# The experts' x in rows of their own, their slots one group ahead, and whole matrices as items

## The chip, the cores and the metric

The kernel runs on one core of a Trainium2 chip; the other seven have nothing to do. The metric is the device time of one launch in microseconds, as the median of several runs. The profile is of one execution. In what follows PE is the matrix engine (TensorE), DVE VectorE, ACT ScalarE, POOL GpSimd and SP the queue that issues most transfers.

## What is computed

256 tokens of 1024 features pass through two blocks of two layers each, all in float32. The first block holds recurrent, attention and MLP layers; it is not touched here. In the second block each of the two layers is a mixer (latent attention in layer 0, pooled means in layer 1), a layer norm, a sum over experts and a layer norm. There are 64 experts, and a token goes to two of them:

```
f = mla_mixer(...) if i == 0 else pool_mixer(...)
x = layer_norm(DEEPNORM_ALPHA * x + f, ln_g[i, 0], ln_b[i, 0])
f = hier_moe(x, ...)                 # gate * (silu(x @ w1[e]) * (x @ w3[e])) @ w2[e], over 2 experts e of 64
x = layer_norm(DEEPNORM_ALPHA * x + f, ln_g[i, 1], ln_b[i, 1])
```

An expert's w1 and w3 are 1024 x 256 and its w2 is 256 x 1024, a mebibyte each. All 64 experts of both layers are computed, so 384 such matrices, 403 MB, come from memory once.

## The kernel before

Each engine's instructions run in the order in which the program writes them. For the experts (function moe) they are done in 16 groups of four, `for g in range(16)`, in each of two layers. An expert has 32 slots for rows, so a group has 128. The steps of a group on PE, with the lines of their products:

- gather (L1406): the rows of the group's tokens are picked and turned in one, by a product of x, which is the stationary operand, with a one-hot matrix G of tokens by slots. DVE makes G of the slots' numbers (L1397). A product takes 128 features of x by 128 slots; there are 8 chunks of features and 2 blocks of tokens, and the trace has two records for each product in float32, so 32. The chunks are those features whose number is the same modulo 8 (`xk = x.rearrange("p b (q k) -> p b k q", k=8)`), because the weights' rows are laid over the partitions as "(p k)". So a chunk of x is read in steps of eight elements.
- up (L1444): products of w1 and w3 with the gathered rows, then tanh and two products on ACT and DVE (L1448 to L1451) that give h.
- back (L1429): G times the gates is Gg (DVE, L1425); two transposes of it make GT, the weighted way back.
- down: two transposes of h (L1459), a copy to hT (ACT, L1461), the products with w2 (L1470) to Y, and the products of GT with Y (L1479) that add into the accumulators of both token blocks.

The order around a group's end is: up of group g, then on DVE G of group g + 1, gather of g + 1, Gg of g + 1, back, and then down of group g. In group GAIN (6) the norm's gain and shift are put on x (affine), and alpha * x is added to the sum (L1586). After the products of group OVER (8) stands the code for experts with more than 32 rows, behind a branch on a number that the router finds; in the profiled execution none of its instructions run.

The weights come as items of 1 MB in the order of use, a list that stream_items writes. For w1 and w3 an item is half of the rows of two experts: `w[l, e:e + 2].rearrange("e (p k) f -> p e (k f)", k=8)[:, :, h * 1024:(h + 1) * 1024]`, in two pieces of 4096 bytes a partition. A w2 item is one expert's matrix, 8192 bytes in a piece. The last four items, w2 of the last group, are quarters of the columns over four experts, in pieces of 1024 bytes. There are 21 slots for items, ten in the pool that the earlier layers used and eleven that come free with the experts' phase. raw_w(key) hands out item i and has item i + 20 issued, so the transfer of an item waits until the item 21 before it has been used. On SP a transfer also waits for one of eight completion counters (DMAHW0 to 7), which are taken in turn. Between the two layers two more items bring the pooling mixer's weights.

Of the kernel before, what the change touches and what calls it, by code (L numbers as in the profile page):

```python
# [9 lines left out]
F32 = mybir.dt.float32  # L10
# [60 lines left out]
def _layout(inputs):  # L71
    """The arrays of the launch: the inputs, the small vectors also laid end to end, constants of the shapes."""
    a = {n: np.ascontiguousarray(inputs[n]) for n in _INS}
    a["rows"] = np.concatenate([a[n].reshape(-1, 128) for n in _ROWS])
    a["brows"] = np.concatenate([a[n].reshape(-1, 128) for n in _BROWS])
    a["wr"] = np.concatenate([a["moe_w_grp_2"], a["moe_w_exp_2"]], -1)
    a["br"] = np.concatenate([a["moe_b_grp_2"], a["moe_b_exp_2"]], -1)
    a["cst"], a["poolm"] = _constants()
    return a


class Kern:
# [6 lines left out]
    # ---------------------------------------------------------------- weights  # L89
    def stream_items(self):  # L90
# [59 lines left out]
        for l in range(2):  # L150
            for g in range(16):
                for h in range(2):
                    for n, w in ((1, A["moe_w1_2"]), (3, A["moe_w3_2"])):
                        for q in range(2):
                            e = 4 * g + 2 * q
                            it.append(((n, l, g, h, q), w[l, e:e + 2].rearrange("e (p k) f -> p e (k f)", k=8)
                                       [:, :, h * 1024:(h + 1) * 1024], (2, 1024)))
# [39 lines left out]
    def tick(self, ahead=1):  # L197
        """half of the next split but one: first hi, then lo."""
# [72 lines left out]
    def g_tok(self, xT, key, outs, n, splitn=1, mid=None):  # L271
        """outs[blk][j]: [128, n]: token rows, from both halves of K."""
# [18 lines left out]
    def g_feat(self, xT, key, mid=None, bank=None, end=None):  # L291
        """[128 features, 2, 256 tokens] twice, for 512 features."""
# [73 lines left out]
    def rsqrt(self, r, n):  # L366
        """r <- r ** -0.5 for r [128, n], n <= 4: a seed from the exponent, then Newton steps."""
# [57 lines left out]
    # ---------------------------------------------------------------- attention over pairs of 64-wide heads  # L425
    def attend(self, ap, pairs, scores, V, mask, outp, yts, sink=None, pre=None):
        """Softmax attention, two heads at a time, three pairs in flight. Gives the prologue and the rest."""
# [69 lines left out]
        def main(pend=None, nxt=None, ahead=1):  # L497
            """The pairs in turn; then the products out of the last are still owed. nxt() makes an attention to go on with."""
# [29 lines left out]
    # ---------------------------------------------------------------- mixer 0  # L528
    def mixer0(self):
        nc, A = self.nc, self.A  # L530
        with ExitStack() as st:
# [30 lines left out]
            def lru():  # L562
                col = self.col
                # halves of the biases, 2 * softplus(-lambda)
# [5 lines left out]
                for hf in range(2):  # L570
# [26 lines left out]
                    # tanh(z/2) = w, z = -log a: a = 2/(1+w) - 1, sqrt(1-a^2) = 2 sqrt(w)/(1+w)  # L597
# [34 lines left out]
            def forget():  # L632
                # log sigmoid, running sums, biases
# [72 lines left out]
    def pair_scores(self, qT, kT):  # L706
        """Heads 2p and 2p+1 in the two halves of the partitions of chunk p."""
# [145 lines left out]
    # ---------------------------------------------------------------- squared relu mlp  # L853
# [35 lines left out]
    # ---------------------------------------------------------------- mixer 1  # L889
    def mixer1(self, xT):  # L890
        nc, A = self.nc, self.A
        x = self.x
        with ExitStack() as st:
# [4 lines left out]
            tab = ap.tile([128, 2, 2, 2, 32], F32, name="tab")     # q or k, block, cos or sin  # L898
# [11 lines left out]
            def rope(dst, src, nh, qk, b):  # L910
                """dst, src [128, nh, 64]."""
# [11 lines left out]
            def feat(dst, tk, nch):  # L923
                """tokens x features (two blocks) to features x tokens."""
# [92 lines left out]
    def stats(self, y):  # L1017
        """mean and 1 / sqrt(var + eps) of a block of rows in parts, in steps: a seed from the exponent, Newton steps."""
# [23 lines left out]
    def both(self, gens):  # L1042
        """the generators' steps in turn; what they return."""
# [11 lines left out]
    def normed(self, y, dst):  # L1055
        """dst <- (y - mean) / sqrt(var + eps); y[block][half]."""
# [5 lines left out]
    def affine(self, g, bb):  # L1062
        """x <- x * g + b."""
        for o, v in ((ALU.mult, g), (ALU.add, bb)):
            for h in range(2):
                for b in range(2):
                    t = self.x[:, b, h * 512:(h + 1) * 512]
                    self.nc.vector.tensor_tensor(t, t, v[h], op=o)

    def router(self, rp):  # L1070
        """the router's weights times the gain of the norm before, less the mean over the rows; its bias plus that of
        the norm's shift. In steps."""
# [22 lines left out]
    def rotary(self):  # L1095
        """tables from the positions: cos, sin [128, block, 16], in steps."""
# [71 lines left out]
            # what dies first comes first: the experts' weights follow into it  # L1168
# [97 lines left out]
            # the residual's own norm  # L1266
# [16 lines left out]
    def warm(self, n):  # L1283
        """products that nothing reads, against the drop of TensorE's clock in a wait."""
# [4 lines left out]
    # ---------------------------------------------------------------- experts  # L1289
    def moe(self, l, wp, bank, y, before_last):  # L1290
        """x becomes the norm's output before gain and shift, of y[block][half]; bank: banks that are free at the start.
        The sum is returned. The router's weights are free of their columns' means, so that it can take y as it is."""
# [8 lines left out]
        # logits, token rows; feature chunk k is k, k + 8, ...  # L1301
        xk = x.rearrange("p b (q k) -> p b k q", k=8)
# [25 lines left out]
        def one_hots(v, n, k):  # L1328
            """the first k of v [128, 2, 8] from the largest on, the first of equals first: one-hot, and values."""
# [32 lines left out]
        def gates():  # L1362
            nonlocal gt, ci
            # gates
# [18 lines left out]
            # further rounds of 32 rows an expert  # L1383
# [10 lines left out]
        def gather(g, s, first=False):  # L1394
            """rows of group g: [128 features, 8, 128 slots], in halves of the features, and the one-hot slots."""
            G = wp.tile([128, 2, 4, 32], F32, name="G", bufs=1)
            tt(G, s[:, :, 4 * g:4 * g + 4, None].to_broadcast([128, 2, 4, 32]),  # L1397
               iota[:, None, None, :].to_broadcast([128, 2, 4, 32]), op=ALU.is_equal)
            Gf = G.rearrange("p b e s -> p b (e s)")
# [20 lines left out]
            return xg, G, half  # L1420

        def back(g, G):
# [386 lines left out]
```

## Time and profile before

| | us |
|---|---|
| runs: median (lowest to highest) | 1929.14 (1928.67 to 1932.13) |
| profiled execution: span from the first to the last instruction | 1926.0 |
| PE busy | 1748.4 (91%) |
| DVE busy | 749.8 (39%) |
| ACT busy | 578.8 (30%) |

The time of the profiled execution as the runs are timed isn't shown; its span lies 3.1 us below their median. The first gather of the experts starts at 920.4 us, so their phase, with the pooling mixer within it, is the last 1005 us. Of the page's groups, the costliest of this phase are the gather (252.5 us on PE, 1024 records), the products with w1 and w3 (235.6 us, 4096), those with w2 (160.6 us, 992) and the way back (118.2 us, 248). Busy time is no measure of what could be saved: an engine that waits is idle in it, and one that is slow is busy. Transfers moved 550.11 MB, 286 GB/s over the span.

### The profile page before, as it was taken

The numbers are of one execution on the slowest core, as the hardware profiler recorded it, in microseconds if no ns is written. First come the engines' busy times: TensorE is split into PE (matmuls) and PEld (weight loads), VectorE is DVE, ScalarE is ACT, GpSimd is POOL, SyncE is SP. The second block draws the span as 40 slices with busy tenths as digits, with TensorE's granted clock in tenths as the row PEclk, the third lists the DMA queues.
The fourth block names the chain that finished last, engine by engine and source line by source line (L and its number), as shares of the span: only waits on it lengthen the run. The fifth ranks groups of instructions, "written<-read, shape, count | busy, mean of one in ns | idle before, by whom it ended". The sixth has DMA issues, their size and how long they took to land. (4 is left out here: it accounts for less than half of the span.)

```text
span 1926.0 us, 29923 instructions
## 1 busy us (share of the span) xinstructions
PE 1748.4 (91%) x12712; PEld 1316.9 (68%) x12712; DVE 749.8 (39%) x1599; ACT 578.8 (30%) x1047; POOL 11.3 (1%) x22
## 2 busy tenths in 40 slices
PE   7999999999999999999888897888998878878886
PEld 7998899989878899877554554555475455545554
DVE  6886576556675655585210111101151111110112
ACT  5644445444564544466111100000021110000001
POOL 0000000000000000000000000000000000000000
PEclk9999999999999999999888889888998879898898
DMA  8544355554524455556899999999989999999993
GB/s 278 179 152 150 117 170 197 187 184 155 196 66 153 147 195 184 177 213 256 341 356 411 415 384 403 409 419 422 418 360 359 378 415 412 386 406 413 422 421 115
DMA packets 160611, 550.11 MB, mean 286 GB/s; under 512 B 9660, under 2 KB 33551, under 8 KB 144463
## 3 DMA queue, kind: packets, MB, share of 16 engines
q1 hardware_dynamic: 158175, 539.18, 73.2%
q0 software_dynamic: 2144, 8.66, 1.2%
q8 instruction: 104, 1.70, 0.3%
q14 instruction: 44, 0.36, 0.0%
q10 hardware_dynamic: 144, 0.21, 0.0%
HBM read 546.97 MB, written 1.05 MB: 285 GB/s over the span
## 5 line engine op out<-in xcount | busy, mean ns | idle before, releaser
L237 DVE TENSOR_TENSOR wl<-wr,wh 128x1024 fp32r<-128x1024 f32 (+4 forms) x268 | 309.5, 1197 | 119.7 <-ACT wh L234 76.1
L1406 PE MATMUL b<-G,x 128*128 128x128 f32 x1024 | 252.5, 418 | 64.6 <-DVE G L1397 64.5
L1406 PEld LDWEIGHTS b<-G,x 128*128 128x128 f32 x1024 | 247.0, 335 | 78.7 <-issue 78.0
L234 ACT ACTIVATE wh<-wr 128x1024 fp32r<-128x1024 f32 (+4 forms) x268 | 265.1, 1037 | 103.9 <-DVE wl L237 72.3
L1444 PE MATMUL b<-wr,xg 128*32 128x256 f32 x4096 | 235.6, 388 | 2.3 <-ACT xg L1414 2.3
L1444 PEld LDWEIGHTS b<-wr,xg 128*32 128x32 f32 x4096 | 129.6, 112 | 113.1 <-issue 28.0
L1470 PE MATMUL b<-wr,hT 128*32 128x512 f32 x992 | 160.6, 806 | 18.0 <-ACT hT L1461 18.0
L320 PE MATMUL a<-wh,yh 128*128 128x512 f32 x416 | 168.0, 404 | 2.7 <-ACT yh L334 2.7
L320 PE MATMUL a<-wh,yl 128*128 128x512 f32 x416 | 165.1, 397 | 0.6 <-DVE yl L335 0.6
L320 PE MATMUL a<-wl,yh 128*128 128x512 f32 x416 | 164.1, 394 | 0.0
L1449 DVE SCALAR_TENSOR_TENSOR th<-th,b 128x256 f32<-128x256 f32 x32 | 13.5, 421 | 326.4 <-ACT th L1448 326.4
L304 PE MATMUL b<-xh,wl 128*128 128x256 f32 x448 | 121.9, 282 | 0.0
L304 PE MATMUL b<-xh,wh 128*128 128x256 f32 x448 | 121.7, 281 | 0.0
L1470 PEld LDWEIGHTS b<-wr,hT 128*32 128x32 f32 x992 | 36.3, 143 | 124.8 <-issue 96.2
L1479 PE MATMUL a<-Y,GT 128*128 128x512 f32 x248 | 118.2, 618 | 0.0
L1448 ACT ACTIVATE th<-b 128x256 f32<-128x256 f32 x32 | 12.3, 384 | 326.9 <-PE b L1444 326.9
L304 PE MATMUL b<-xl,wh 128*128 128x256 f32 x448 | 110.3, 282 | 0.0
L1475 DVE COPY Y<-b 128x512 f32<-128x512 f32 x31 | 21.4, 692 | 206.9 <-PE b L1470 206.9
L320 PEld LDWEIGHTS a<-wh,yh 128*128 128x128 f32 x416 | 78.1, 188 | 23.3 <-ACT yh L334 4.5
L1479 PEld LDWEIGHTS a<-Y,GT 128*128 128x128 f32 x248 | 42.0, 189 | 75.7 <-issue 30.5
L320 PEld LDWEIGHTS a<-wh,yl 128*128 128x128 f32 x416 | 78.1, 188 | 22.5 <-DVE yl L335 3.9
L304 PE MATMUL a<-xh,wh 128*128 128x256 f32 x320 | 90.0, 290 | 1.5 <-ACT xh L348 1.1
(460 smaller groups left out, 2533.2 us busy)
## 6 DMA issues: line engine op xcount, KB each, us to landing
wr<-in_moe_w SPq DMA_DIRECT2D x372, 1024.0 KB, 15.4
wr<-in_mlp_w_up SPq DMA_DIRECT2D x32, 1024.0 KB, 5.3
wr<-in_mlp_w_down SPq DMA_DIRECT2D x32, 1024.0 KB, 4.9
wr<-in_xa_w_kv SPq DMA_DIRECT2D x16, 1024.0 KB, 5.3
wr<-in_xa_w_q SPq DMA_DIRECT2D x8, 1024.0 KB, 4.9
wr<-in_xa_w_o SPq DMA_DIRECT2D x8, 1024.0 KB, 5.0
wr<-in_cd_w_in SPq DMA_DIRECT2D x8, 1024.0 KB, 4.9
wr<-in_moe_w POOLq DMA_DIRECT2D x8, 1024.0 KB, 7.2
```

Source lines behind the costliest of these rows:

```text
L234: nc.scalar.activation(hi[:, s], r[:, s], AF.Copy)
L237: nc.vector.tensor_tensor(lo[:, s], r[:, s], hi[:, s].bitcast(F32), op=ALU.subtract)
L304: nc.tensor.matmul(o[f // 2][:, f % 2, :], wt[c][:, kk, f * 128:(f + 1) * 128], xT(a, h * 4 + kk), start=(h == 0 and kk == 0 and a == 0 an ...
L320: nc.tensor.matmul(acc[b][hf], yT[a][:, chunk, b * 128:(b + 1) * 128], wt[c][:, j, hf * 512:(hf + 1) * 512], start=(first and a == 0 and c ...
L1406: nc.tensor.matmul(ps[:, k], xk[:, b, 4 * i + k], Gf[:, b], start=(b == 0), stop=(b == 1))
L1444: nc.tensor.matmul(ps[32 * e:32 * e + 32, which], xg[:, k, 32 * e:32 * e + 32], w(e, k), start=(which == 0 and k == 0), stop=(k == 7), ski ...
L1448: nc.scalar.activation(th, ps[:, 0], AF.Tanh, scale=0.5)
L1449: stt(th, th, 1.0, ps[:, 0], op0=ALU.add, op1=ALU.mult)
L1470: nc.tensor.matmul(y[hf][32 * e:32 * e + 32], hT[:, c, 32 * e:32 * e + 32], w(c)[:, hf * 512:(hf + 1) * 512], start=(c == 0), stop=(c == 1 ...
L1475: nc.vector.tensor_copy(Y[:, 512:], y[1])
L1479: nc.tensor.matmul(acc[b][hf], GT[:, b * 128:(b + 1) * 128], Y[:, hf * 512:(hf + 1) * 512], start=first, stop=end, skip_group_check=True)
```

## The change

There are four parts. Comments and doc strings are dropped as well, which moves the lines' numbers.

1. x is kept in another order of columns in the experts' phase: chunk k of the features lies in 128 columns of its own. So the gather and the router's transposes read x in a row, and the steps that write x or take it by halves (the copy ahead of the router, affine, the product with alpha) go over it in steps of 128 elements.
2. G and Gg of group g + 2 are made on DVE at the end of group g's down, one group earlier. For this G and Gg are functions of their own (slots, weighted).
3. The transposes of h (turned, out of down) stand between gather and back.
4. An item of w1 or w3 is a whole matrix of one expert, 8192 bytes a partition. The order of products in up is now w1, first half of the rows, w1, second half, w3, w3, where it was w1, w3, w1, w3; and four items are taken at once.

```diff
@@ stream_items
-                for h in range(2):
-                    for n, w in ((1, A["moe_w1_2"]), (3, A["moe_w3_2"])):
-                        for q in range(2):
-                            e = 4 * g + 2 * q
-                            it.append(((n, l, g, h, q), w[l, e:e + 2].rearrange("e (p k) f -> p e (k f)", k=8)
-                                       [:, :, h * 1024:(h + 1) * 1024], (2, 1024)))
+                for n, w in ((1, A["moe_w1_2"]), (3, A["moe_w3_2"])):
+                    for e in range(4):
+                        it.append(((n, l, g, e), w[l, 4 * g + e].rearrange("(p k) f -> p k f", k=8), (8, 256)))
@@ affine
-    def affine(self, g, bb):
+    def affine(self, g, bb, half=None, as_=lambda t: t):
+        half = half or (lambda b, h: self.x[:, b, h * 512:(h + 1) * 512])
...
-                    t = self.x[:, b, h * 512:(h + 1) * 512]
-                    self.nc.vector.tensor_tensor(t, t, v[h], op=o)
+                    t = half(b, h)
+                    self.nc.vector.tensor_tensor(t, t, as_(v[h]), op=o)
@@ moe
-        xk = x.rearrange("p b (q k) -> p b k q", k=8)
+        xk = x.rearrange("p b (k q) -> p b k q", k=8)
+        xn = x.rearrange("p b (k q) -> p b q k", k=8)
+        half_x = lambda b, h: xn[:, b, 64 * h:64 * h + 64]
+        by8 = lambda t: t.rearrange("p (q k) -> p q k", k=8)
...
-                nc.scalar.activation(x[:, b, h * 512:(h + 1) * 512], y[b][h], AF.Copy)
+                nc.scalar.activation(half_x(b, h), by8(y[b][h]), AF.Copy)
@@ moe, parts
-            def get(n, h):
+            def get(n):
+                w = []
+
                 def f():
-                    w = [self.raw_w(n, l, g, h, q) for q in range(2)]
-                    return lambda e, k: w[e // 2][:, e % 2, (k % 4) * 256:(k % 4 + 1) * 256]
+                    if not w:
+                        w.extend(self.raw_w(n, l, g, e) for e in range(4))
+                    return lambda e, k: w[e][:, k]
                 return f
-            return [(n // 2, range(4 * h, 4 * h + 4), get(n, h)) for h in range(2) for n in (1, 3)]
+            return [(n // 2, range(4 * h, 4 * h + 4), f) for n, f in ((1, get(1)), (3, get(3))) for h in range(2)]
@@ moe, the loop over groups
             if g < 15:
-                xg, G, half = gather(g + 1, s1, g < GAIN)
+                xg, half = gather(G, g < GAIN)
                 if g:
                     half(1)
-                    GT = back(g + 1, G)
+            if g != OVER:
+                hT = turned(h)
+            if 0 < g < 15:
+                GTn = back(Gg)
...
+            if g < 14 and g != OVER - 1:
+                G = slots(g + 2, s1)
+                Gg = weighted(g + 2, G)
             if g < 15:
+                GT = GTn
                 h = up(g + 1, xg, parts(g + 1), fill=fill)
```

Three places show what stands where. The first is DVE around the end of up of group 2 in layer 0, where h is the group's activation, xg the gathered rows and Y the products with w2. Before:

```order
L1449 SCALAR_TENSOR_TENSOR th<-th,b 128x256 [waits Activation_49]
L1451 SCALAR_TENSOR_TENSOR h<-th,b 128x128x2 [waits DVE_49]
L1397 TENSOR_TENSOR G<-r_s_8831,keep 128x256
L1412 TENSOR_SCALAR xg<-b,pcol 128x128 [waits Activation_49] x4
L1425 TENSOR_TENSOR Gg<-G,r_gt 128x256 [waits DVE_49]
L1475 COPY Y<-b 128x512 [waits PE_49]
L1449 SCALAR_TENSOR_TENSOR th<-th,b 128x256 [waits Activation_49]
```

With the change:

```order
L1486 COPY Y<-b 128x512 [waits PE_49]
L1398 TENSOR_TENSOR G<-r_s_8831,keep 128x256
L1404 TENSOR_TENSOR Gg<-G,r_gt 128x256 [waits DVE_49]
L1457 SCALAR_TENSOR_TENSOR th<-th,b 128x256 [waits Activation_49]
L1459 SCALAR_TENSOR_TENSOR h<-th,b 128x128x2 [waits DVE_49]
L1422 TENSOR_SCALAR xg<-b,pcol 128x128 [waits Activation_49] x4
L1486 COPY Y<-b 128x512 [waits PE_49]
```

G stood behind h and Gg behind the copies of xg, each just ahead of the products on PE that read it. Both now stand behind the copy of Y, ahead of the activations th and h of a group that comes before their use.

The second place is PE at the end of up of group 1 in layer 0: gather of group 2 (G, x), transposes of Gg and of h, and the first products with w2 (wr holds an item). Before:

```order
L1406 MATMUL b<-G,x 128x128 x16
L1429 MATMUL b<-keep,Gg 128x128 x2
L1459 MATMUL b<-keep,h 128x128 x2
L1470 MATMUL b<-wr_8692,hT 32x512
L1470 MATMUL b<-wr,hT 32x512 x3
L1470 MATMUL b<-wr_8692,hT 32x512
```

With the change:

```order
L1416 MATMUL b<-G,x 128x128 x16
L1466 MATMUL b<-keep,h 128x128 x2
L1437 MATMUL b<-keep,Gg 128x128 x2
L1481 MATMUL b<-wr_8692,hT 32x512
L1481 MATMUL b<-wr,hT 32x512 x3
L1481 MATMUL b<-wr_8692,hT 32x512
```

The transposes of h are now ahead of those of Gg. The number of products is the same.

The third place is PE in group 0 of layer 0, with the product of ones in which the router counts rows (r_M). Before:

```order
L1406 MATMUL b<-G,x 128x128 x8
L1444 MATMUL b<-wr,xg 32x256 x32
L1385 MATMUL b<-r_M,ones 128x64 x2
L1406 MATMUL b<-G,x 128x128 x8
L1444 MATMUL b<-wr,xg 32x256 x32
```

With the change:

```order
L1416 MATMUL b<-G,x 128x128 x8
L1452 MATMUL b<-wr,xg 32x256 x16
L1386 MATMUL b<-r_M,ones 128x64 x2
L1416 MATMUL b<-G,x 128x128 x8
L1452 MATMUL b<-wr,xg 32x256 x48
```

The first half of w3 stood ahead of the second half of the gather; now only the first half of w1 does, and no item has been used up at that point, since an item of w1 serves both halves.

## Rows read from the trace of the kernel before

**Rows 1.** The page: span of the profiled execution.
```profile
span 1926.0 us, 29923 instructions
```

**Rows 2.** Stretches: us, busy of each engine (instructions), PE's clock, DMA share, GB/s.
```profile
932.00:1400.00 468.00, 397.63 (x3228) 236.56 (x3228) 62.22 (x132) 44.62 (x99) 0.00 (x0) 0.87 0.99 401
1510.00:1880.00 370.00, 314.01 (x2528) 190.36 (x2521) 45.98 (x96) 33.76 (x74) 0.00 (x0) 0.88 1.01 411
```

**Rows 3.** PE's waits in 1510 to 1880: for whom, us in total, times, longest.
```profile
PE b L1406 <- DVE G L1397: 28.8, 13, 4.3
PE b L1429 <- DVE Gg L1425: 19.1, 12, 2.4
```

**Rows 4.** Waits of SP's queue in 850 to 1926, the same columns.
```profile
SPq L180 <- PE b L1470: 285.8, 30, 17.5
SPq L180 <- DMA wr<-in_moe_w: 105.9, 76, 3.3
```

**Rows 5.** One group on PE: start, us, engine, line, operation, idle before it.
```profile
1760.64 7.86 PE L1406 MATMUL b<-G,x 128*128 128x128 f32 x32 [1.96 <-DVE G L1397]
1769.70 0.41 PE L1429 MATMUL b<-keep,Gg 128*128 128x128 f32 x2 [1.21 <-DVE Gg L1425]
1770.86 5.24 PE L1470 MATMUL b<-wr,hT 128*32 128x512 f32 x32 [0.53 <-ACT hT L1461]
1776.04 3.81 PE L1479 MATMUL a<-Y,GT 128*128 128x512 f32 x8
1779.78 7.11 PE L1444 MATMUL b<-wr,xg 128*32 128x256 f32 x128
```

**Rows 6.** Loads of x on PE (ns min/median/max), and eight products of the mixer.
```profile
L1406 PEld LDWEIGHTS b<-G,x x1024: 312/336/341, 920.3 to 1881.6; 128*128 128x128 f32 x171
...
L1618 PEld LDWEIGHTS a<-wr,x x16: 190/192/192, 1407.8 to 1411.3; 128*128 128x128 f32 x16
...
L1311 PEld LDWEIGHTS a<-keep,x x16: 187/193/207, 1421.4 to 1423.5; 128*128 128x128 f32 x16
...
1408.01 1.05 PE L1618 MATMUL a<-wr,x 128*128 128x128 f32 x8
```

**Rows 7.** Short stretches by kind of item: w2, w1/w3, between layers, the last four.
```profile
1820.00:1827.50 7.50, 5.76 (x25) 5.20 (x23) 1.02 (x2) 1.37 (x3) 0.00 (x0) 0.73 1.01 425
1800.00:1817.50 17.50, 15.54 (x171) 7.01 (x164) 1.97 (x4) 0.98 (x2) 0.00 (x0) 0.96 1.03 420
1400.00:1432.50 32.50, 31.43 (x205) 27.43 (x203) 19.98 (x83) 10.35 (x16) 0.00 (x0) 1.00 1.02 423
1880.00:1887.50 7.50, 5.76 (x30) 3.34 (x33) 1.02 (x2) 0.77 (x2) 0.00 (x0) 0.77 1.07 365
1887.50:1895.00 7.50, 7.50 (x101) 4.15 (x93) 0.69 (x1) 1.79 (x3) 0.00 (x0) 1.00 0.35 121
```

**Rows 8.** Starts: layer 0's first group, between the layers, after the branch, the end.
```profile
920.37 4.08 PE L1406 MATMUL b<-G,x 128*128 128x128 f32 x16 [0.94 <-DVE G L1397]
925.06 3.75 PE L1444 MATMUL b<-wr,xg 128*32 128x256 f32 x64 [0.61 <-ACT xg L1414]
...
1393.79 3.64 PE L1470 MATMUL b<-wr,hT 128*32 128x512 f32 x32 [0.53 <-ACT hT L1461]
...
1432.73 1.66 PE L1406 MATMUL b<-G,x 128*128 128x128 f32 x6 [0.94 <-DVE G L1397]
...
1711.96 0.42 DVE L1397 TENSOR_TENSOR G<-r_s,keep 128x256 f32<-128x256 f32 x1 [6.46 <-PEq L1525]
...
1911.17 1.07 PE L1500 MATMUL b<-wr,hT 128*32 128x256 f32 x16
```

**Rows 9.** Stretches with the transfers in part idle: layer 0's start, layer 1's start.
```profile
925.00:927.50 2.50, 2.44 (x44) 1.15 (x48) 1.61 (x9) 0.78 (x4) 0.00 (x0) 1.00 0.18 75
927.50:930.00 2.50, 2.50 (x34) 1.78 (x24) 1.48 (x10) 0.00 (x0) 0.00 (x0) 1.00 0.78 233
1432.50:1442.50 10.00, 9.16 (x88) 6.99 (x89) 3.33 (x20) 1.23 (x4) 0.00 (x0) 1.00 0.37 139
```

More of the change, by code (lines that the diff above doesn't have):

```diff
@@ L1392, in gates, with slots @@
             nc.vector.tensor_copy(ci, cm)
-        def gather(g, s, first=False):
+        def slots(g, s):
             G = wp.tile([128, 2, 4, 32], F32, name="G", bufs=1)
@@ L1398, in gather, with weighted @@
                iota[:, None, None, :].to_broadcast([128, 2, 4, 32]), op=ALU.is_equal)
+            return G
+        def weighted(g, G):
+            Gg = wp.tile([128, 2, 4, 32], F32, name="Gg", bufs=1)
+            tt(Gg, G, gt[:, :, 4 * g:4 * g + 4, None].to_broadcast([128, 2, 4, 32]), op=ALU.mult)
+            return Gg
+        def gather(G, first=False):
             Gf = G.rearrange("p b e s -> p b (e s)")
@@ L1419, in gather, with back @@
             half(0)
-            return xg, G, half
-        def back(g, G):
-            Gg = wp.tile([128, 2, 4, 32], F32, name="Gg", bufs=1)
-            tt(Gg, G, gt[:, :, 4 * g:4 * g + 4, None].to_broadcast([128, 2, 4, 32]), op=ALU.mult)
+            return xg, half
+        def back(Gg):
             Gg = Gg.rearrange("p b e s -> p b (e s)")
@@ L1453, in up, with turned @@
             return h
-        def down(g, h, GT, acc, getw2, first, end, fill=()):
+        def turned(h):
             ps = self.pb([128, 2, 128])
@@ L1461, in down @@
             nc.scalar.activation(hT, ps, AF.Copy)
+            return hT
+        def down(g, hT, GT, acc, getw2, first, end, fill=()):
             if getw2 is None:
@@ L1549, in overflow, with mid @@
                     for g in range(16):
-                        xg, G, half = gather(g, s2)
+                        G = slots(g, s2)
+                        xg, half = gather(G)
                         half(1)
-                        GT = back(g, G)
+                        GT = back(weighted(g, G))
                         h = up(g, xg, parts2(g))
-                        down(g, h, GT, acc, lambda: getw2(g), False, False)
-        xg, G, half = gather(0, s1, True)
-        h = up(0, xg, parts(0), lambda: (gates(), half(1)))
-        GT = back(0, G)
+                        down(g, turned(h), GT, acc, lambda: getw2(g), False, False)
+        G = slots(0, s1)
+        xg, half = gather(G, True)
+        Gg = []
+        def mid():
+            nonlocal G
+            gates()
+            half(1)
+            Gg.append(weighted(0, G))
+            G = slots(1, s1)
+        h = up(0, xg, parts(0), mid)
+        GT = back(Gg.pop())
+        Gg = weighted(1, G)
         acc = self.pacc()
         for g in range(16):
-            this = h, GT
             w2g = lambda: [((0, 1), [(e, w2(l, g, e)) for e in range(4)])]
             if g == OVER:
-                down(g, *this, acc, w2g, False, False)
+                down(g, turned(h), GT, acc, w2g, False, False)
                 overflow()
+                G = slots(g + 1, s1)
+                Gg = weighted(g + 1, G)
             if g == GAIN:
-                self.affine(self.bc(2 * l), self.bc(4 + 2 * l))
+                self.affine(self.bc(2 * l), self.bc(4 + 2 * l), half_x, by8)
+            GTn = None
             if g < 15:
-                xg, G, half = gather(g + 1, s1, g < GAIN)
+                xg, half = gather(G, g < GAIN)
                 if g:
                     half(1)
-                    GT = back(g + 1, G)
+            if g != OVER:
+                hT = turned(h)
+            if 0 < g < 15:
+                GTn = back(Gg)
             fill = []
@@ L1578, in moe @@
             if g != OVER:
-                down(g, *this, acc, None if (l, g) == (1, 15) else w2g, g == 0, g == 15, fill)
+                down(g, hT, GT, acc, None if (l, g) == (1, 15) else w2g, g == 0, g == 15, fill)
             if g == 0:
                 half(1)
-                GT = back(1, G)
+                GTn = back(Gg)
             if g == GAIN:
@@ L1585, in moe @@
                     for hf in range(2):
-                        nc.tensor.matmul(acc[b][hf], self.alpha_id, x[:, b, hf * 512:(hf + 1) * 512], start=False, stop=False,
+                        nc.tensor.matmul(acc[b][hf], self.alpha_id, half_x(b, hf), start=False, stop=False,
                                          skip_group_check=True)
+            if g < 14 and g != OVER - 1:
+                G = slots(g + 2, s1)
+                Gg = weighted(g + 2, G)
             if g < 15:
+                GT = GTn
                 h = up(g + 1, xg, parts(g + 1), fill=fill)
```

## The prediction, made before the changed kernel ran

> **What bounds the kernel now.** I read the page's head first, then the experts' phase by stretches, since the change touches nothing ahead of it. The span is 1926.0 us [rows 1]. In two long stretches of that phase the DMA engines are busy all the time, yet they move 401 and 411 GB/s on the mean, and PE is busy 85% of them at a granted clock of 0.87 to 0.88 of 2.4 GHz [rows 2]. So two things are near their limit together. To see which one waits, I took PE's waits: in 1510 to 1880 they are for G (28.8 us, 13 times) and Gg (19.1 us, 12 times), both made on VectorE after the activations [rows 3]. None is for a transfer. From the other side, SP, which issues the weights, waits 285.8 us for the w2 products to free a buffer, and only 105.9 us for an earlier transfer [rows 4]. The experts' phase is therefore a chain on PE, and the transfers follow it with buffers that come free late.
>
> One group on PE reads so [rows 5]: gather 7.86 us after a wait of 1.96, then a wait of 1.21 for Gg, transposes 0.41 (and the like for h), a wait of 0.53 for hT, w2 products 5.24, way back 3.81, w1 and w3 products 7.11, which end at 1786.9. With the next wait for G that makes 28.2 us from gather to gather. The gather is odd: its weight loads have a median of 336 ns, where those of the pooling mixer, also 128x128 out of x but in a row, have 192 ns, and eight of the latter's products take 1.05 us, 131 ns each, where the gather's 32 take 246 ns each [rows 5, 6].
>
> The other limit: a group brings 12 items of 1.0486 MB, 12.58 MB. While the queue is well filled, w1/w3 items (pieces of 4096 bytes) run at 420 GB/s and w2 items (8192 bytes in a piece) at 425. I told the two apart by counting items back from the stream's end, and [rows 7] has one stretch of each of three like ones (424 to 425, 419 to 420). At 425 a group costs 29.6 us.
>
> **What the change does, part by part.**
>
> *The gather's x.* 32 records at 131 ns are 4.2 us, from 7.9: 3.7 us less on PE in each group. A bound from the other side: the router's transposes also load the strided x, at 193 ns [rows 6]; if stride were not the reason, the gain would be nothing. The Trainium skill (SBUF — State Buffer, "Door 1: The DMA port swizzle") says that lines of SBUF are 16 bytes and each access that crosses to a new one pays, and float32 in steps of eight crosses each time. The 336 against 192 ns agrees with it, the transposes' 193 don't; I take 4.2, because the pooling mixer's rows are the same form of matmul.
>
> *G and Gg a group ahead.* Both waits, 1.96 and 1.21 us, go. What is late next: the transposes of h need h, made some 2 us after the last w3 product, and the gather of 4.2 us covers that; back's transposes stand between them and the w2 products and cover most of hT's 0.53. The DVE work is only moved: it lies under the way back now. If that cover were gone it would cost the two waits again.
>
> *PE's group afterwards.* 4.2 + 0.41 + 0.41 + 0.1 + 3.64 + 3.81 + 7.11 = 19.7 us at the full clock (3.64 is the w2 products in an undisturbed group [rows 8]). With the gather unchanged it would be 23.4. Both are below 29.6: **the transfers become the bound**, and what PE gains beyond that is lost in waits for them. So I don't sum the gains on PE; I follow the stream of bytes.
>
> *The stream.* 384 items of 1.0486 MB and 1.84 MB for the pooling mixer are 404.5 MB. The first 21 items land as before while the router runs. Then every slot is full until one is freed. Now that happens early: the first 16 products of w1 free two items near 926.9, and after a dip to 75 GB/s the next 2.5 us have 233, which puts the first new bytes at 928.6, 1.7 us later [rows 8, 9]. With the change, four items of w1 are freed together, behind the gates and the second half of the gather. From the first gather at 920.37 [rows 8]: half a gather 2.1, the first evacuation 0.6 (from 924.45 to 925.06), 16 products of w1 1.9, four records with ones 0.5 (at no more than 131 ns), half a gather 2.1, and some 2.4 for the four evacuations and the last products (an estimate: four times the first's 0.6): 930. With the 1.7 us to the first bytes the stream resumes at 932. Copies into a strided x stand ahead of this; they write the same elements with a step, for which there is no row, and I take nothing, with 2.4 us (four copies at the evacuation's 0.6, doubled) as the other bound.
>
> Left then: 404.5 - 22.0 = 382.5 MB, of which the last four items (4.2 MB, pieces of 1024 bytes, unchanged) go at 365 GB/s [rows 7]: 11.5 us. The other 378.3 MB are all in pieces of 8192 bytes. At 425 they take 890.1 us. Bounds: 411 and 401, the means of the present stretches [rows 2], give 920 and 943; 433, an estimate from 425 plus the 5 to 8 that it gained over the smaller pieces, gives 874.
>
> *Holes in it.* Between the layers no item is consumed. The 21 slots are then all in flight or landed; they last 21 x 2.467 = 51.8 us after the last w2 item of layer 0. PE starts those products at 1393.79 and the next layer's gather at 1432.73 [rows 8], 38.9 us; with 1.7 us from landing to start, the 9.6 us from gather to first release as above and 1.7 to the first bytes that makes 51.9. So the hole nearly closes: 2 us with slower copies, bounds nothing and 8. It is 10 us at 139 GB/s now [rows 9]. Two other stalls stay, the branch over the overflow code (6.46 us on VectorE [rows 8]) and the norm's gain and shift, now on strided x. PE has 29.6 - 19.7 = 9.9 us to spare in a group, and SP up to eight transfers issued ahead (19.7 us), so I cost both at nothing; with the cover gone each is some 6 us, twice.
>
> *SP's order.* Items are issued in the order of use, 21 ahead, as before. What stands behind a w1 item that isn't free yet is only the next item, whose slot is freed later anyway. That four are needed where two were is a wait of PE for data in the same stream; only a last item's wait reaches the end.
>
> *The tail.* Now the stream ends near 1890 and PE some 36 us later, because PE is behind it [rows 7]. Afterwards PE is level with the stream: from the landing of the last quarter of w2, 1.7 us, then the 14.8 us from 1911.17 to the end [rows 8], and 1.8 us more if the last products run at 1.2 GHz after a wait.
>
> **Sum:** 932 + 890.1 + 11.5 + 2 + 1.7 + 14.8 + 1.8 = 1853.9 us of span. The profiled execution's span, 1926.0, lies 3.1 us under the median 1929.14; I add these: **1857 us**, 72 less. By origin: some 47 us are holes and thin stretches of the present stream, 7 us its piece size (890.1 against 897 at a mean of 421.7), 18 us the tail.
>
> **The rivals.**
>
> *The stream stays thin* (its mean goes to 411, not 425). Speaking for it: these stretches have a DMA share of 0.99 and 1.01 and still no 420 [rows 2]. Against: from 1400 to 1432.5, where PE takes nothing and the queue is full, it ran at 423 [rows 7]. It adds 30 us: **1887**, chance 0.11. At 401, **1910**, chance 0.04. Faster than forecast, at 433 and without a hole: **1839**, chance 0.06.
>
> *PE at its lower clock becomes the bound, and the kernel gets slower.* Waits for data are new on PE. The mean granted clock is 0.73 and 0.77 in stretches where PE is busy for 5.76 of 7.5 us, so a half of them is at 1.2 GHz, and 0.96 to 1.00 where it is busy nine tenths [rows 7]. If all of a group ran at 1.2 GHz it would take up to 2 x 19.7 = 39.4 us, 11 more than now, over 32 groups 350 us: near 2280. It decides from the point at which PE's group passes the present 28 to 30 us, that is, if over half of its work is at 1.2 GHz all the time. Against it: as soon as PE falls behind, it has up to 13 landed items before it, works without a gap, and such stretches have the full clock. At a mean of 0.73, 19.7 us become some 27, still under 29.6. The Trainium skill (TensorE: Matmul & The Clock Gate, "Avoid throughput drops mid-kernel") warns of just this, gaps in which PE waits for a transfer. Chance 0.03.
>
> *No change.* The engines are all busy already, so a faster PE might only wait. Then 411 and the present holes stay, but the tail's 18 us go all the same: 1911. To come out at 1929, the stream would have to be slower with 8192 bytes than with 4096, and it is faster [rows 7]. Chance 0.02. [...]
>
> **How the numbers follow.** Forecast (stream at 418 to 432) 0.74: 1857, own range 1843 to 1873. Rivals as above: 0.11, 0.04, 0.06, 0.03, 0.02. The range 1838 to 1890 leaves out 0.04 + 0.03 + 0.02 and half of the fast case. Three runs of the kernel differ by 0.2%, about what a measurement can tell from no change. Faster by more: 0.95; within: 0.02; slower: 0.03.
>
> **What would show it.** The gather's 32 records near 4.2 us and weight loads near 190 ns; waits for G and Gg gone, and PE's products of w1, w3 or w2 waiting for transfers in most groups; DMA at 420 to 430 GB/s from some 935 to the last four items, with at most a short dip near 1430; SP waiting for transfers rather than for products; the last transfer landing 18 to 20 us ahead of the end, near 1835. Wrong would be: a stream with dips in every group while slots are free, a gather still at 7.9 us together with a clock near 0.6, or a stream that resumes long after 935.

## The result, and the profile after

The changed kernel takes 1861.53 us (median of four runs, 1860.07 to 1862.93), the one before 1928.91 beside it: a ratio of 0.965, 95% interval 0.9637 to 0.9664, 67.4 us less. The prediction was 1857. The page of the changed kernel, with the transfers' rate over 40 slices of the span, and its shares of the chain that ended last:

```profile
span 1859.4 us, 29896 instructions
GB/s 288 182 159 123 127 166 197 184 191 176 181 108 136 114 184 190 192 159 230 272 405 427 425 427 425 426 426 426 421 425 398 426 426 426 426 424 427 426 427 237
PE 54%; DMA 39%; DVE 3%; ACT 3%; issue 1%; SPq 0%; DVEq 0%; ACTq 0%
```

From slice 22 to the last but one the transfers run at 421 to 427 GB/s, but for the 398 in slice 31, and they are now 39% of the chain. Stretches (columns as in [rows 2]):

```profile
920.00:940.00 20.00, 16.78 (x208) 10.52 (x212) 7.50 (x30) 3.99 (x11) 0.00 (x0) 1.00 0.57 227
932.00:1335.00 403.00, 328.16 (x3004) 172.63 (x2997) 60.32 (x116) 40.68 (x94) 0.00 (x0) 0.92 1.01 426
1400.00:1440.00 40.00, 35.99 (x416) 23.20 (x415) 12.75 (x46) 7.08 (x18) 0.00 (x0) 1.00 0.95 394
1430.00:1820.00 390.00, 312.17 (x2882) 162.92 (x2874) 57.09 (x109) 37.73 (x87) 0.00 (x0) 0.92 1.01 426
...
930.00:932.50 2.50, 2.50 (x52) 1.56 (x48) 0.28 (x1) 0.00 (x0) 0.00 (x0) 1.00 0.46 125
1345.00:1350.00 5.00, 2.55 (x22) 1.11 (x26) 0.00 (x0) 0.00 (x0) 0.00 (x0) 0.69 0.97 367
1407.50:1415.00 7.50, 6.95 (x104) 4.63 (x108) 3.70 (x18) 0.92 (x2) 0.00 (x0) 1.00 0.69 256
1825.00:1837.50 12.50, 12.50 (x132) 7.33 (x131) 0.99 (x2) 2.77 (x5) 0.00 (x0) 1.00 1.01 351
1837.50:1840.00 2.50, 1.97 (x31) 1.06 (x34) 0.04 (x1) 0.54 (x2) 0.00 (x0) 1.00 0.49 171
```

The two long stretches have 426 GB/s where [rows 2] had 401 and 411. The short ones show where the stream resumes, a dip, the hole between the layers, the last four items and the end. Waits of PE, and then of SP, in 850 to 1860:

```profile
PE b L1452 <- DMA wr<-in_moe_w: 114.5, 71, 3.1
PE b L1481 <- ACT hT L1468: 22.3, 30, 1.5
PE b L1416 <- DVE G L1398: 10.7, 4, 4.5
PE b L1416 <- DVE x L1066: 9.1, 4, 4.2
PE b L1481 <- DMA wr<-in_moe_w: 5.1, 6, 1.4
```

```profile
SPq L177 <- DMA wr<-in_moe_w: 685.1, 331, 3.4
SPq L177 <- PE b L1452: 54.8, 14, 19.1
...
SPq L177 <- PE b L1481: 15.4, 16, 5.8
```

PE waited for G and Gg before [rows 3], and now for transfers; G is left with four waits (two first groups, two branches). SP waited for products [rows 4], and now for transfers. The roles have changed over. One group on PE, to be held against [rows 5], and the gather's loads against [rows 6]:

```profile
953.90 3.84 PE L1416 MATMUL b<-G,x 128*128 128x128 f32 x32
957.57 0.38 PE L1466 MATMUL b<-keep,h 128*128 128x128 f32 x2
957.79 0.38 PE L1437 MATMUL b<-keep,Gg 128*128 128x128 f32 x2
959.50 3.64 PE L1481 MATMUL b<-wr,hT 128*32 128x512 f32 x32 [1.32 <-ACT hT L1468]
963.07 3.80 PE L1490 MATMUL a<-Y,GT 128*128 128x512 f32 x8
```

```profile
L1416 PEld LDWEIGHTS b<-G,x x1024: 186/192/338, 920.5 to 1809.4; 128*128 128x128 f32 x171
```

With 7.11 us for w1 and w3 that is 20.0 us a group when the data are there.

### The profile page after: what moved, and what is told of

Read it like the earlier page. It is cut to its first block, busy times and chain, and to the rows that moved or that the text cites. A ratio compares the mean times of both kernels' runs of the same rounds, so it can differ in the third digit from the quotient of the medians.

```text
span 1859.4 us, 29896 instructions
## 1 busy us (share of the span) xinstructions
PE 1651.3 (89%) x12712; PEld 1200.5 (65%) x12712; DVE 760.3 (41%) x1599; ACT 577.9 (31%) x1047; POOL 10.2 (1%) x22
## 4 chain that ended last, share of the span: by engine, by line
PE 54%; DMA 39%; DVE 3%; ACT 3%; issue 1%; SPq 0%; DVEq 0%; ACTq 0%
DMA wr<-in_moe_w 38%; PE a L317 16%; PE b L301 9%; PE a L301 5%; PE b L1452 3%; PE a L280 3%; PE b L741 3%; PE b L1416 2%; PE a L741 2%; PE b L1481 1%; PE b L481 1%; PE b L470 1%; DVE x L1066 1%; PE a L1490 1%; ACT wh L231 1%
## 5 line engine op out<-in xcount | busy, mean ns | idle before, releaser
L1452 PE MATMUL b<-wr,xg 128*32 128x256 f32 x4096 | 308.1, 424 | 116.8 <-DMA wr<-in_moe_w 114.5
L1452 PEld LDWEIGHTS b<-wr,xg 128*32 128x32 f32 x4096 | 147.7, 121 | 282.9 <-DMA wr<-in_moe_w 152.9
L1481 PE MATMUL b<-wr,hT 128*32 128x512 f32 x992 | 124.7, 598 | 27.5 <-ACT hT L1468 22.3
L1416 PE MATMUL b<-G,x 128*128 128x128 f32 x1024 | 131.5, 289 | 19.8 <-DVE G L1398 10.7
L1416 PEld LDWEIGHTS b<-G,x 128*128 128x128 f32 x1024 | 124.9, 202 | 33.3 <-issue 17.1
L317 PEld LDWEIGHTS a<-wl,yh 128*128 128x128 f32 x416 | 78.2, 188 | 17.2
```

What stands on the lines that cost most here:

```text
L317: nc.tensor.matmul(acc[b][hf], yT[a][:, chunk, b * 128:(b + 1) * 128], wt[c][:, j, hf * 512:(hf + 1) * 512], start=(first and a == 0 and c ...
L1416: nc.tensor.matmul(ps[:, k], xk[:, b, 4 * i + k], Gf[:, b], start=(b == 0), stop=(b == 1))
L1452: nc.tensor.matmul(ps[32 * e:32 * e + 32, which], xg[:, k, 32 * e:32 * e + 32], w(e, k), start=(which == 0 and k == 0), stop=(k == 7), ski ...
L1481: nc.tensor.matmul(y[hf][32 * e:32 * e + 32], hT[:, c, 32 * e:32 * e + 32], w(c)[:, hf * 512:(hf + 1) * 512], start=(c == 0), stop=(c == 1 ...
```

## The experiments

The theory T is the prediction's: the stream of weights binds as soon as PE's group is shorter than the 29.6 us that its 12 items take; time that PE saves beyond that is spent in waits.

**Each part alone, on the kernel before.** Part 1 (x_only), parts 2 and 3 (slots_only) and part 4 (items_only) of the change. Of x_only the core is

```diff
-        xk = x.rearrange("p b (q k) -> p b k q", k=8)
+        xk = x.rearrange("p b (k q) -> p b k q", k=8)
```

with the copy, affine and the product with alpha to match; the others are the hunks of the loop over groups, and those of stream_items and parts.

> The kernel before with the chunkwise x alone. Theory T (the stream of weights becomes the bound as soon as PE's group is shorter than the 29.6 us that its 12 items need; what PE gains beyond that is lost in waits): the gather's 32 records fall to 4 us, PE's group from 28.2 to 24.5 us, so the whole gain but that of the piece size comes with this part alone: 1865 to 1873 us, stream at 420 to 423 GB/s, PE waiting for transfers although G and Gg are still waited for. Rival R1 (PE stays the chain that sets the time, the parts add up by the PE time they save, 3.7 us a group here and 3.2 by the slots): 36 of the 67 us, 1893. Rival R2 (the piece size carries the gain): 1925 or more.

> The kernel before with the slots a group ahead (and h turned ahead of the way back) alone; x and the items as before. T: PE's group falls from 28.2 to 25.0 us, below 29.6, and the stream binds: 1867 to 1876 us, gather still at 7.9 us, PE waiting for transfers. R1: 31 of the 67 us, 1898. R2: 1925 or more.

> The kernel before with whole matrices as items alone; gather and waits for G and Gg as before. T: PE's chain of some 31 us a group at its mean clock still binds, the pieces of 8192 bytes change nothing: 1922 to 1933 us. R1: the same. R2 (the piece size carries the gain): 1900 or less.

Measured: x_only 1863.98 us (0.9656, 0.9641 to 0.9671), slots_only 1866.19 (0.9673, 0.9658 to 0.9688), items_only 1926.74 (0.9989, 0.9978 to 1.0001). Either of the two cuts on PE brings nearly the whole gain alone, 65 and 63 us, and together they bring 66 (no_items, below; 67 with part 4): R1, by which they add up, falls. R2 falls with items_only, which changes nothing that can be measured. Waits of PE in x_only:

```profile
PE b L1409 <- DVE G L1400: 68.3, 30, 5.6
PE b L1432 <- DVE Gg L1428: 53.8, 32, 2.4
PE b L1447 <- DMA wr<-in_moe_w: 34.9, 26, 3.0
```

There PE still waits 122 us for G and Gg, and it costs next to nothing, since it would otherwise wait for transfers. In items_only there is no wait of PE for a transfer at all, and in spite of its larger pieces the stream is nearly as thin as before, 405 GB/s where the kernel before has 399 in the same stretch:

```profile
932.00:1335.00 403.00, 339.06 (x2793) 203.47 (x2794) 52.19 (x111) 38.71 (x86) 0.00 (x0) 0.86 0.98 405
```

So the thin rate of [rows 2] was PE's doing. x_only and slots_only came 1 us below their ranges. Their streams resume earlier (337 and 279 GB/s from 920 to 940 us, 227 in the changed kernel), which the ranges left out; the next runs show that the old items do this. No run separates part 2 from part 3.

**All parts but one, on the changed kernel.** no_items undoes part 4, no_x part 1, no_slots parts 2 and 3.

```diff
-                    for e in range(4):
-                        it.append(((n, l, g, e), w[l, 4 * g + e].rearrange("(p k) f -> p k f", k=8), (8, 256)))
+                        for q in range(2):
+                            e = 4 * g + 2 * q
+                            it.append(((n, l, g, h, q), w[l, e:e + 2].rearrange("e (p k) f -> p e (k f)", k=8)
+                                       [:, :, h * 1024:(h + 1) * 1024], (2, 1024)))
```

> The changed kernel with the items of before (4096 bytes a partition). T: the stream binds and its mean rate falls from 425.5 to 421.7 GB/s, 8.6 us over 378 MB; the first release comes some 3 us earlier, since two items are freed by half of w1: 1864 to 1869 us. Rival (rate of the items does not matter, PE or the holes set the time): 1857 to 1862, the earlier release alone. R2: 1890 or more.

> The changed kernel with x strided as before (slots ahead and whole matrices are kept). T: PE's group is 20.0 + 3.9 = 24 us, below the 29.6 of its 12 items, so PE only waits less for transfers: 1859 to 1866 us, no more than 0.2% from the changed kernel. R1 (gains of PE add up): 1897.

> The changed kernel with G and Gg made where they were before, and h turned after (chunkwise x and whole matrices are kept). T: PE's group is some 24.5 us, below 29.6: 1859 to 1867 us; the waits for G and Gg are back in the list of PE's waits, and those for transfers are shorter by as much. R1: 1893.

Measured: no_slots 1862.65 us (0.9655, 0.9642 to 0.9668), level with the changed kernel, with 123 us of waits for G and Gg back on PE: T as expected, though PE's waits for transfers fall only from 119.6 to 38.9 us, not by the whole 123. no_items 1862.81 (0.9656, 0.9643 to 0.9669), level too, though T gave 1864 to 1869. no_x 1869.03 (0.9692, 0.9678 to 0.9705), 7.5 us over the changed kernel, where T gave at most 4.5. Stretches of no_items:

```profile
920.00:940.00 20.00, 17.11 (x212) 10.66 (x216) 7.27 (x30) 4.03 (x11) 0.00 (x0) 1.00 0.88 338
932.00:1335.00 403.00, 331.42 (x3000) 170.62 (x2990) 60.31 (x116) 40.67 (x94) 0.00 (x0) 0.94 1.02 420
1400.00:1440.00 40.00, 36.00 (x416) 23.23 (x415) 13.31 (x52) 6.65 (x17) 0.00 (x0) 1.00 1.02 418
1430.00:1820.00 390.00, 319.05 (x2902) 162.02 (x2904) 57.51 (x110) 38.15 (x88) 0.00 (x0) 0.94 1.02 422
```

The smaller pieces do cost 4 to 6 GB/s within the groups. But half of w1 frees two items where now all of w1 frees four, so the stream resumes earlier in layer 0 and has no hole between the layers: (338 - 227) x 20 and (418 - 394) x 40 GB/s x us are 3.2 MB, 7.5 us at 426. Part 4 gives with one hand and takes with the other. The same two places show what x is worth; of no_x:

```profile
920.00:940.00 20.00, 18.84 (x179) 14.45 (x179) 6.31 (x27) 2.80 (x8) 0.00 (x0) 1.00 0.42 167
...
1400.00:1440.00 40.00, 35.99 (x267) 25.12 (x266) 10.89 (x48) 4.76 (x13) 0.00 (x0) 0.96 0.88 365
```

That is 60 x 20 and 29 x 40 GB/s x us, 2.4 MB or 5.5 us, of the 5.7 by which no_x's profiled span (1865.1) is the longer; its median is 7.5 higher. I had priced the slow gather against PE's slack within a group, and forgotten that two halves of it stand ahead of each layer's first release, where nothing covers them.

**How much PE has to spare.** Products of 128x128 that nothing reads are added on PE in 30 groups, 32 or 64 in each.

```diff
             if g < 15:
+                self.warm(32)
                 GT = GTn
```

> The changed kernel with 32 products of 128x128 added on PE ahead of the w1 products of each group but the first of a layer (30 groups, the sums are untouched); 64 records of 120 ns are 7.7 us a group. T: 20.0 + 7.7 = 27.7 us is still below 29.6, the added work takes the place of waits for transfers: 1861 to 1870 us. Rival R1 (PE's chain sets the time): 30 x 7.7 = 230 us more, 2092.

> The same with 64 products, 15.4 us a group. T: 20.0 + 15.4 = 35.4 us is above 29.6, PE becomes the bound by 5.8 us in each of 30 groups: 1861 + 174 = 2035, 2015 to 2055 us, with the stream at some 355 GB/s. R1: 30 x 15.4 = 462 us more, 2323. If the clock falls to 1.2 GHz in half of the work, 2250 or more.

Measured: pe_32 1872.2 us (0.9704, 0.969 to 0.9719), so of the 219 us added (30 times 7.31) only 10.7 show; pe_64 2083.15 (1.0801, 1.0784 to 1.0817). The slack is real and R1 falls in both, but both lie above T's ranges: the slack is smaller than T's 9.6 us a group (29.6 less 20.0). In pe_32 waits for transfers are nearly gone (1.4 us), and its stream has lost a little everywhere: 424 and 422 GB/s in the two long stretches and 381 between the layers, 7 us in all against the changed kernel; and the end comes some 26 us after the stream's rather than 20.7, since PE is behind. In pe_64 one undisturbed group, from one series of added products to the next, takes 33.2 us (34.2 in the groups ahead of GAIN):

```profile
1243.85 14.46 PE L1285 MATMUL b<-keep 128*128 128x128 f32 x128
1258.24 7.11 PE L1452 MATMUL b<-wr,xg 128*32 128x256 f32 x128
...
1277.02 1.17 PE L1285 MATMUL b<-keep 128*128 128x128 f32 x9
```

That is less than the 35.4 expected, so the total's miss lies elsewhere: I had added to a time in which the branch, the norm's gain and shift and the start of each layer are covered by the stream, and once PE binds nothing covers them. From one series of added products to the next it is 51.4 and 50.7 us over the norm's gain and shift, and 41.5 and 43.9 over the branch: 17 us and 8 to 11 more than the groups beside them, where the prediction had put some 6 on each with the cover gone. What PE had to spare in all can be read from PE's rows for the whole phase. Against the changed kernel, pe_64 has 433.8 us of added products, 119.6 us of waits for transfers less, and products with w1 and w3 that take 229.0 us in place of 308.1 and with w2 114.6 in place of 124.7, at a granted clock of 0.99 in place of 0.92. That leaves 225 us, and the span grew by 221.6. So PE's slack was 209 us, 7.0 for each of the 30 groups, and the 7.3 of pe_32 had already used it up.

**Slots.**

```diff
-        self.ring2_n = 11
+        self.ring2_n = 9
```

> The changed kernel with 19 slots in place of 21 for the items of the experts. T: at the start of each layer's experts two items fewer lie ready or in flight, and the stream stands idle for 2 x 2.47 = 4.9 us more, once ahead of the first group and once between the layers; within the groups nothing changes, since PE has some 10 us to spare in each: 1862 + 10 = 1872, 1868 to 1876 us, with the stream still at 425 GB/s within the groups. Rival (the slots do not limit, the stream is the chip's alone): 1860 to 1863. Rival (the spare slots within groups hold the rate up): 1885 or more, with 415 GB/s or less in long stretches.

Measured: 1872.38 us (0.97, 0.9682 to 0.9719), 10.9 over the changed kernel. The stream has 426 GB/s within the groups as ever. The two missing items show at both starts. In layer 0 it has 335 and 179 GB/s from 900 to 920 and from 920 to 940, where the changed kernel has 389 and 227: 4.8 us at 426. At the hole between the layers, against 394, it loses 6.9 us:

```profile
1400.00:1440.00 40.00, 35.99 (x388) 24.71 (x392) 16.67 (x79) 9.90 (x21) 0.00 (x0) 1.00 0.77 321
```

Together these are 11.6 of the 12.0 us by which its profiled span is the longer. So a slot is worth some 2.4 us at the first start and 3.4 at the second, and nothing elsewhere.

**Both kinds of items.**

```diff
+                if g == 0:
+                    for h in range(2):
+                        for n, w in ((1, A["moe_w1_2"]), (3, A["moe_w3_2"])):
+                            for q in range(2):
...
+                else:
                     for n, w in ((1, A["moe_w1_2"]), (3, A["moe_w3_2"])):
                         for e in range(4):
```

> The changed kernel, with the first group of each layer alone in the items of before (halves of the steps of two experts, 4096 bytes a partition), all other groups in whole matrices. The kernel with the items of before in all groups came out level with the changed kernel (ratios 0.9656 and 0.965), and its stream has 420 and 422 GB/s instead of 426 within the groups, but 338 instead of 227 GB/s from 920 to 940 us and 418 instead of 394 from 1400 to 1440. Theory T2 (the piece size is worth its 7 to 9 us, but freeing four whole matrices at once gives as much back at the two starts): (338 - 227) x 20 + (418 - 394) x 40 = 3.2 MB, or 7.5 us at 426, come back, less 1 us for two groups at 420: 1853 to 1857 us, 0.25 to 0.45% below the changed kernel. Rival (the end of the kernel does not follow the stream's bytes): 1860 to 1863 us.

Measured: 1854.69 us (0.9618, 0.9602 to 0.9634), 6.8 below the changed kernel and, with tail_mixed below, the fastest of all: T2 as expected. Its stretches have the early start of the one and the rate of the other:

```profile
920.00:940.00 20.00, 16.36 (x202) 10.78 (x206) 7.93 (x31) 4.03 (x11) 0.00 (x0) 1.00 0.84 340
932.00:1335.00 403.00, 330.64 (x3052) 171.86 (x3052) 61.51 (x119) 40.74 (x94) 0.00 (x0) 0.92 1.01 426
1400.00:1440.00 40.00, 35.79 (x414) 22.50 (x418) 12.19 (x41) 8.59 (x22) 0.00 (x0) 1.00 1.01 421
```

**The end.** In the changed kernel PE waits for a transfer for the last time ahead of 1820.28, and works on, but for 0.53 us for hT, up to the last quarter of w2, which it starts 5.8 us after the stream's end (taken by the rate, see the sum below). Its rows there, and stretches with the clock and the rate:

```profile
1820.28 3.62 PE L1452 MATMUL b<-wr,xg 128*32 128x256 f32 x26 [1.44 <-DMA wr<-in_moe_w]
1823.83 2.49 PE L1008 MATMUL b<-brow,keep 128*128 128x128 f32 x16
...
1844.51 1.07 PE L1511 MATMUL b<-wr,hT 128*32 128x256 f32 x16
```

```profile
1820.00:1822.50 2.50, 2.22 (x24) 1.07 (x25) 0.00 (x0) 0.00 (x0) 0.00 (x0) 0.50 1.02 429
1822.50:1825.00 2.50, 2.50 (x16) 1.44 (x9) 0.00 (x0) 0.00 (x0) 0.00 (x0) 0.54 1.01 416
...
1840.00:1842.50 2.50, 2.50 (x32) 1.20 (x24) 0.00 (x0) 0.61 (x2) 0.00 (x0) 1.00 0.04 13
```

The products with brow (L1008) belong to the last norm and stand there as work to fill a wait. I moved them out from between the products with w1 and w3, on the changed kernel and on the version with both kinds of items.

```diff
             if g == 14 and l == 1:
-                fill = [lambda i=i: before_last(i) for i in range(2)]
+                fill = [None]
             if g != OVER:
                 down(g, hT, GT, acc, None if (l, g) == (1, 15) else w2g, g == 0, g == 15, fill)
+                if fill:
+                    fill.pop(0)
+                    for i in range(2):
+                        before_last(i)
```

> The changed kernel with the 32 products that spread the last norm's gain and shift over the partitions (4.5 us on PE) ahead of the last group's w1 products instead of between them, and the two deferred products of the way back one part earlier. In the changed kernel PE waits for no transfer after 1820.28 and starts the last w2 quarter at 1844.51, while the stream ends near 1839: theory T3 (at the end it is PE that is late, not the last four items at some 350 GB/s) has the 4.5 us move under the waits of 4.1 us that stand ahead of 1820.28: w2 starts some 3 us earlier, 1857 to 1859.5 us. Rival (the last transfers set the end): 1860 to 1863 us.

> The same edit on the version whose first groups alone have the items of before. T3: again some 3 us less than that version's 1854.7: 1850 to 1853 us. Rival: 1853 to 1856 us.

Measured: tail_only 1861.07 us (0.9636, 0.9623 to 0.9649) and tail_mixed 1855.9 (0.9613, 0.9599 to 0.9626), neither to be told from its original. T3 falls. In tail_only a new wait stands where the work was, and for w3, not for the last four items:

```profile
1823.55 1.91 PE L1452 MATMUL b<-wr,xg 128*32 128x256 f32 x26 [1.13 <-DMA wr<-in_moe_w]
...
1831.08 0.63 PE L1452 MATMUL b<-wr,xg 128*32 128x256 f32 x6
1833.50 3.64 PE L1452 MATMUL b<-wr,xg 128*32 128x256 f32 x58 [1.79 <-DMA wr<-in_moe_w]
...
1839.74 3.56 PE L1511 MATMUL b<-wr,hT 128*32 128x256 f32 x32 [0.53 <-ACT hT L1468]
```

PE came earlier to w3's products and found a matrix missing. So at the end PE and the stream are level, and the filling work lay where it cost nothing. One execution of each shows a little more than the medians. From the arrival of w3's last matrix to the end it is some 29 us in the changed kernel, 28.6 in tail_only and 26.9 in tail_mixed. In tail_only the clock is 0.50 from 1840 to 1842.5, and the 32 records that take 3.56 us there take 1.93 in the other two. What the edit gains after w3 is thus at most some 2 us, and the medians don't show it.

## Why the prediction was right, and where it was off

The mechanism was right: the transfers became the bound, what PE saved beyond that went into 119.6 us of waits for them, and the rate is that of a filled queue. The sum, term by term, on the profiled execution:

| term | predicted | measured |
|---|---|---|
| stream resumes | 932 | 931.8 |
| 378.3 MB | 890.1 | 892.0 |
| hole between the layers | 2 | 3.0 |
| last four items | 11.5 | 11.9 |
| end of the stream to the last quarter's products | 1.7 | 5.8 |
| from there to the end | 14.8 | 14.9 |
| lower clock at the end | 1.8 | within the 5.8 |
| span | 1853.9 | 1859.4 |

The stream resumes 0.7 us ahead of 932.5 (125 GB/s in the stretch before). The hole is 7.5 us at 256 instead of 426 GB/s. The last 4.19 MB went at 351, and the end, 1838.7, follows from 171 GB/s in the last stretch; as in the prediction it is an end by the rate, and a few last packets still move after 1840. What is left for the 378.3 MB is 892.0 us, a mean of 424; the dip at 1345 is 0.7 of the 1.9 us above the forecast. There a part of the trace's packets has 1024 and 6144 bytes: they are the pooling mixer's two items, which the prediction counted among the pieces of 8192 bytes. The rest was not located. From span to median I added 3.1, and 2.1 was right.

*The step that failed* is the tail: "from the landing of the last quarter of w2, 1.7 us", for which no row stood, took the last transfer for the last thing that is late. PE reaches that quarter 5.8 us after the stream's end and doesn't wait for it; what is late is the whole chain from w3's last matrix on. The 1.8 us for a low clock were of the right size but stood in the wrong place. The clock is 1.00 from 1825 to 1847.5, but 0.50 and 0.54 from 1820 to 1825, after the last waits: the 26 records of products with w1 take 3.62 us there, and 1.91 in tail_only at 1.00. With the first products with brow that makes some 2 us, ahead of w3's last matrix, where tail_only shows that time saved on PE is lost again in a wait.

*The gather* fell to 3.84 us where I took 4.2, and its loads to a median of 192 ns, so the stride was the reason. The rule of the Trainium skill (SBUF — State Buffer, "Door 1: The DMA port swizzle") on lines of 16 bytes bore out. The transposes' 193 ns with strided x [rows 6], which the prediction counted against it, are no exception. They were slow too, as the same loads with x in a row show:

```profile
L1312 PEld LDWEIGHTS b<-keep,x x16: 138/140/143, 908.8 to 911.3; 128*128 128x128 f32 x16
```

It is 140 or 141 ns in every run with x in a row, and 192 or 193 in slots_only and no_x. To compare a strided load with one of another kind of product was the mistake; why the transposes' loads are the faster ones in both cases no run tells.

*hT* was not covered: 1.32 us in the group shown, 22.3 in all, against 18.3 in no_slots, where h is turned later; the prediction had 0.1 us. That the group still came to 20.0 against 19.7 is in part luck, since the gather came out 0.4 shorter. The wait lies in PE's slack, and nothing here shows a gain from part 3.

*The origin of the gain* was told wrongly in one point. "7 us its piece size" is the right size for the rate (no_items against the changed kernel), but it is no part of what the change gained: the same part delays both starts by as much. I had the late release in the sum (932 for 928.6), and did not set it against the piece size. The tail gave some 15 us rather than 18, from 36 to 20.7; the rest of the 67 us is holes and thin stretches.

*The rivals.* A stream that stays thin (0.15 in all) is excluded by items_only and x_only: it was thin while PE was late. The lower clock stayed a small matter: PE waits 77 times for a transfer, and its granted clock in the long stretches is 0.92, up from 0.87. The Trainium skill's warning of such gaps (TensorE: Matmul & The Clock Gate, "Avoid throughput drops mid-kernel") is seen in 1345 to 1350, 0.69. PE waits for the stream there, so no cost shows; over the phase the products with the weights ran 89 us longer than in pe_64, and that went into PE's slack.

## What to carry to other kernels

When two resources are near their limit, take PE's time for a round and the transfers' time for the same round from rows of undisturbed ones, and forecast the larger; gains on the other side don't add up, and either of two cuts may do alone. What the other side has to spare is read over the whole phase and not from one undisturbed round: it was 7.0 us a group here, not 9.6. Then look at where the cover is missing, the starts and the end of the stream: there a slow gather, two slots or the grain in which buffers are freed each cost 7 to 11 us, while 219 us of added products elsewhere cost 11. Large pieces for the rate and small ones where a stream has to restart can be had together.

## What the runs showed of the hardware

Pieces of 8192 bytes a partition ran at 426 GB/s, and a stream with two thirds of its items in pieces of 4096 (no_items) at 420 to 422, over stretches of 400 us with a full queue. The Trainium skill (DMA: Bandwidth & Descriptors, "Where 436 GB/s comes from") has the memory's side bind at some 358 GB/s for a core; here, with one core at work, it did not.

Stepping through float32 costs also where it isn't the stationary operand. In the changed kernel the products with alpha take x as the moving operand in steps, the copies write x in steps on ACT, and affine reads and writes it in steps on DVE:

```profile
L1616 PE MATMUL a<-x,keep x16: 1024/1040/1042, 1107.6 to 1595.2; 128*128 128x512 f32 x16
...
L1310 ACT ACTIVATE x<-a x4: 1076/1103/1137, 906.7 to 909.4; 128x512 f32<-128x512 f32 x4
...
L1066 DVE TENSOR_TENSOR x<-x,b x24: 681/1004/1031, 1087.0 to 1575.3; 128x512 f32<-128x512 f32 x24
```

Before, the same had medians of 592, 598 and 676 ns. None of it was seen in the time: the products lie in PE's slack, as do the 9.1 us for which PE waits for affine's x, and the first gather starts at 920.52, against 920.37 [rows 8], although four of the copies stand ahead of it.
